# Attention row maxima: negated scores, and a second minimum that starts from the first one's value

## The chip, the cores and the metric

The kernel runs on one core of a Trainium2 chip. The metric is device time in microseconds (us), the median of several runs. Engines are named as in the profile: PE is TensorE's matmuls, PEld its weight loads, DVE VectorE, ACT ScalarE, POOL GpSimd, SP the engine that issues DMAs. A line such as L201 is a line of the kernel's source.

## The reference, cut to what matters

The reference is one layer of a backbone with two branches on the same normalised input: chunked gated linear attention, and differential attention. The change touches the second. For each of 8 heads there are two components, each with its own queries and keys (64 wide, normalised and rotated), and one value matrix. There are 1024 queries, and 1280 keys (256 of context, 1024 latent).

```python
scale = d ** -0.5                               # 1/8
s1 = jnp.einsum('bhqd,bhkd->bhqk', qb1, k1).astype(jnp.float32) * scale
s2 = jnp.einsum('bhqd,bhkd->bhqk', qb2, k2).astype(jnp.float32) * scale
a = jax.nn.softmax(s1, axis=-1) - lam * jax.nn.softmax(s2, axis=-1)
return jnp.einsum('bhqk,bhkv->bhqv', a.astype(v.dtype), v)
```

The queries are `rms_norm(q) * q_gain` before the rotation, so a factor on `q_gain` is a factor on every score. A softmax subtracts each row's maximum before the exponential; the maximum itself cancels from the result.

## The kernel before, in words

The program has three phases that overlap at their seams: A (projections and the linear attention, up to about 900 us), B (differential attention, about 900 to 1430 us) and C (the branch projections and the output, to the end).

**Order of the work.** The instructions of PE, ACT, DVE and POOL stand in an order that the program works out while it is built. A class `Driver` (from L59) keeps a clock for each engine and runs small tasks written as generators: each task yields a time, an event, or `On(t, engine)`, which holds it back until that engine's modelled queue is within a microsecond of free. Among tasks that are due, the lowest `prio` goes first. Each instruction on ACT, DVE and POOL is issued by `Engine.emit` (L201), which also gives it a modelled cost, so all of them bear that one line in the profile; matmuls are issued by `mm` (L349), transposes by `tr` (L375), DMAs by `dma` (L314). `banked` adds, for instructions that touch the same PSUM bank from different engines, a wait on the latest earlier one, and takes away waits between different banks. `acq` and `rel` hand out buffers by tag. The engines execute their lists in order. `att_order` writes out by hand the order on PE of the scores S, the transposes T of the exponentials and the product A with the values: the scores run four or five query tiles ahead, so that in the step in which a pair of tiles is multiplied by the values, scores are laid for the tiles that are five and six after the pair's first. Between them `fill` puts matmuls of other products (tile name mb), paced by how many query tiles have been scored.

**A query tile.** There are 64 of them (8 heads, 8 tiles of 128 queries). One PSUM buffer of five banks, `s5`, holds the scores of both components: component 0's first 1024 keys in banks 0 and 1 (main part), component 0's last 256 keys and component 1's first 256 in bank 2 (tail), component 1's other 1024 in banks 3 and 4 (main part). `att_scores` issues component 0's main matmuls, the two tails, and component 1's main matmuls, and spawns the following tasks:

- `att_max`, three times: a DVE reduction of a main part (128 x 1024 to 128 x 1) or of both tails at once (128 x 2 x 256 to 128 x 2), which gives the negated maximum.
- `att_exp`, once for each component: it waits for both reductions that bear on it, joins the two values with a minimum of 128 x 1 on DVE, and issues the ACT exponential of 1280 columns with the joined value as bias. The exponential also gives the row's sum `z`, and its end frees the component's banks for the next tile's scores.
- `att_mix`: after both exponentials, DVE works out the factor of component 1 and mixes the two (the 1280-column instruction e<-e,sm,e).

Afterwards `att_tr` transposes the mixed tile on PE, ACT, POOL and DVE split it into two parts (at), `att_av` multiplies by the values for two tiles at a time, and `att_fin` normalises the result (b1k) and stores it. The small buffers of 128 x 1 and 128 x 2 come from one ring, `sm`, of 48. Four are taken in `att_scores` for a tile (the tails' two maxima, the two main maxima, the sums), one in `att_mix`, and two in `att_fin` for two tiles.

**The gains.** `consts_late` loads the query norm weights and multiplies them by 0.125 on POOL, once, at the start of the program (L475). The rotation tables are multiplied by them later.

Of the kernel before, what the change touches and what calls it, by code (L numbers as in the profile page):

```python
# [13 lines left out]
AF = mybir.ActivationFunctionType  # L14
ALU = mybir.AluOpType
AX = mybir.AxisListType
# [4 lines left out]
P = 128  # L21
# [3 lines left out]
T = S + CTX  # L25
# [207 lines left out]
class Hybrid:  # L233
# [222 lines left out]
    def consts_late(self):  # L456

        nc, a = self.nc, self.a

        def bc(ap, n):  # L460
            return ap.unsqueeze(0).to_broadcast([P, n])

        self.gains = g = self.c("gains", [P, 2, 2, 64])
        for i, nm in enumerate(("diff_q_norm", "diff_k_norm")):
            self.dma(g[:, i, 0], bc(a[nm][0], 64))
        self.ggla = self.c("ggla", [P, 256])
        self.dma(self.ggla, bc(a["gla_norm"][0], 256))
        self.gdif = self.c("gdif", [P, P])
        self.dma(self.gdif, bc(a["diff_norm"][0], P))
        yield from self.acq("p", 2)  # L470
        lp = self.t("p", [P, 4, 64])
        self.dma(lp, a["diff_lambda"][0].unsqueeze(0).to_broadcast([P, 4, 64]))
        yield self.d.when(lp)

        self.pool.tensor_scalar(g[:, 0, 0], g[:, 0, 0], 0.125, 0.0, ALU.mult, ALU.add)  # L475
        for i in range(2):
            gi, gr = (g[:, i, x].rearrange("p (x h e) -> p x h e", h=2, e=16) for x in range(2))
            for hh in range(2):
                self.pool.tensor_scalar(gr[:, :, hh], gi[:, :, 1 - hh], 1.0, 0.0, ALU.mult, ALU.add)
        self.pool.tensor_scalar(self.ggla, self.ggla, 0.5, 0.0, ALU.mult, ALU.add)  # L480
        self.pool.tensor_scalar(self.gdif, self.gdif, 1.0 - LAM_INIT, 0.5, ALU.mult, ALU.mult)
        lm = self.t("p", [P, 2, 64])
        self.dve.tensor_tensor(lm, lp[:, 0::2], lp[:, 1::2], ALU.mult)
        ls = self.c("ls", [P, 2])
        self.rel("p", self.dve.tensor_reduce(ls, lm, AX.X, ALU.add), 2)
        yield self.d.when(ls)
        yield self.act.activation(ls, ls, AF.Exp)
        self.nlam = self.c("nlam", [P, 1])
        self.dve.tensor_tensor(self.nlam, ls[:, 1:2], ls[:, 0:1], ALU.subtract)
        self.dve.tensor_scalar(self.nlam, self.nlam, LAM_INIT, None, ALU.subtract)  # L490
# [1449 lines left out]
    def att_scores(self):  # L1940

        nc, d = self.nc, self.d
        yield self.ev_b
        s5 = self.t("s5", [P, 2 * T])
        for hd in range(8):
            for qt in range(8):
                pr, qs = qt // 2, slice((qt % 2) * P, (qt % 2) * P + P)
                yield self.ev_k[hd]
                yield self.ev_q[hd, pr]
                K, Q = self.K[hd], self.Q[hd, pr]  # L1950

                def score(po, comp, o, n):
                    bank = po.offset % (2 * T) // 512
                    for j in range(2):
                        e = self.mm(po, Q[comp][:, j, qs], K[comp][:, o:o + n], j == 0, j == 1)
                        self.banked(self.ins, "PE", bank)
                    return e

                u = dict(hd=hd, qt=qt, E=[None, None], mt=self.t("sm", [P, 2]), mx=[self.t("sm", [P, 1]) for _ in range(2)],
                         z=self.t("sm", [P, 2]), left=2, ev=[Event() for _ in range(3)])  # L1960

                for comp in range(2):
                    yield from self.acq(f"s{comp}")
                    pm = s5[:, 1536 * comp:1536 * comp + 1024]
                    if comp == 0:
                        yield from self.turn("S", 8 * hd + qt, 0)
                    if self.flush:
                        self.flush(1)
                    for x, (o, n) in enumerate(self.MAIN[comp]):
                        e = score(pm[:, x * 512:(x + 1) * 512], comp, o, n)  # L1970
                        if x == 0:
                            yield AtPE(0)
                    self.passed("S", 8 * hd + qt, comp)
                    d.spawn(self.att_max(u["ev"][comp], u["mx"][comp], pm, 3 * comp, 3 * comp + 1), On(e, "DVE"), prio=-3)
                    yield AtPE(0)
                    if comp == 0:
                        yield from self.acq("st")
                        yield from self.turn("S", 8 * hd + qt, 1)
                        pt = s5[:, 1024:1536].rearrange("p (c k) -> p c k", c=2)
                        for x in range(2):  # L1980
                            e = score(pt[:, x], x, *self.TAIL[x])
                        d.spawn(self.att_max(u["ev"][2], u["mt"], pt, 2), On(e, "DVE"), prio=-3)
                    elif qt == 7:
                        self.rel("kk", e, 2)
                    d.spawn(self.att_exp(u, comp, s5), On(e, "DVE"), prio=-3)
                    yield AtPE(0)
                if qt % 2 == 1:
                    self.rel(*(("aq", e, 2) if hd or pr else ("raw", e)))
                d.set(self.ev_u[8 * hd + qt])

    def att_max(self, ev, mx, pm, *banks):
        self.dve.tensor_reduce(mx, pm, AX.X, ALU.max, negate=True)
        self.banked(self.dve.ins, "DVE", *banks)
        self.d.set(ev)
        return
        yield

    def att_exp(self, u, comp, s5):
        d, mx = self.d, u["mx"][comp]
        yield u["ev"][2]  # L2000
        yield u["ev"][comp]
        yield d.on("DVE", mx)
        self.dve.tensor_scalar(mx, mx, u["mt"][:, comp:comp + 1], None, ALU.min)
        yield self.ev_sb
        yield from self.acq("e5")
        E = u["E"][comp] = self.t("e5", [P, T])
        yield d.on("ACT", mx)
        e = self.act.activation(E, s5[:, 1280 * comp:1280 * comp + T], AF.Exp, bias=mx, accum_out=u["z"][:, comp:comp + 1])
        self.banked(self.act.ins, "ACT", *range(2 * comp, 2 * comp + 3))
        self.rel(f"s{comp}", e)  # L2010
        u["left"] -= 1
        if u["left"] == 0:
            self.rel("st", e)
            if (u["hd"], u["qt"]) == (7, 7):
                d.set(self.ev_s2)
            d.spawn(self.att_mix(u), On(e, "DVE"), prio=self.PM)
# [794 lines left out]
```

## Time and profile before

| | |
|---|---|
| Time, median of 3 runs | 1617.41 us (1617.14 to 1617.72) |
| Span of the profiled execution, first to last instruction | 1614.1 us |
| That execution's own time | not listed; the median is 3.3 us above its span |
| PE busy over the span | 1591.4 us (99%) |
| PEld, DVE, ACT, POOL busy over the span | 82%, 76%, 52%, 39% |
| PE, DVE, ACT, POOL busy in the attention stage (900 to 1430 us) | 524.4, 441.4, 322.3, 323.9 us of 530 |
| Granted TensorE clock | 1.00 throughout |

How to read it: matmuls are pipelined and their ends are modelled, so PE counts as busy a little beyond the point at which the next matmul could have started, and a short wait of PE can be hidden in a busy share. Idle time of another engine costs nothing by itself. A wait is put down to the instruction that came last by the profile.

### The profile page before, as it was taken

The numbers are of one execution on the slowest core, as the hardware profiler recorded it, in microseconds if no ns is written. First come the engines' busy times: TensorE is split into PE (matmuls) and PEld (weight loads), VectorE is DVE, ScalarE is ACT, GpSimd is POOL, SyncE is SP. The second block draws the span as 40 slices with busy tenths as digits, with TensorE's granted clock in tenths as the row PEclk, the third lists the DMA queues.
The fourth block names the chain that finished last, engine by engine and source line by source line (L and its number), as shares of the span: only waits on it lengthen the run. The fifth ranks groups of instructions, "written<-read, shape, count | busy, mean of one in ns | idle before, by whom it ended". The sixth has DMA issues, their size and how long they took to land.

```text
span 1614.1 us, 24349 instructions
## 1 busy us (share of the span) xinstructions
PE 1591.4 (99%) x8229; PEld 1328.1 (82%) x8229; DVE 1224.4 (76%) x2118; ACT 835.7 (52%) x1720; POOL 634.3 (39%) x663
## 2 busy tenths in 40 slices
PE   8999999999999999999999999999999999999999
PEld 3788888888888888888888788888888888888887
DVE  4787945676777779767677688878778888888994
ACT  4776523435343454555535566665665666656331
POOL 1500000001415667535564256656765666560000
PEclk9999999999999999999999999999999999999999
DMA  8576996998878367564645944545587545347662
GB/s 305 201 257 239 329 304 232 344 331 295 278 238 281 116 194 235 167 212 118 189 118 158 253 121 121 151 129 151 150 264 218 159 137 150 111 155 285 204 206 100
DMA packets 259565, 331.16 MB, mean 205 GB/s; under 512 B 22600, under 2 KB 160752, under 8 KB 259440
## 3 DMA queue, kind: packets, MB, share of 16 engines
q1 hardware_dynamic: 259440, 329.60, 63.8%
q8 instruction: 65, 1.06, 0.3%
q14 instruction: 60, 0.49, 0.1%
HBM read 225.20 MB, written 104.33 MB: 204 GB/s over the span
## 4 chain that ended last, share of the span: by engine, by line
PE 89%; DVE 4%; issue 2%; DMA 2%; ACT 1%; POOL 1%; SPq 0%; ACTq 0%; DVEq 0%; POOLq 0%
PE mm L349 30%; PE mb L349 11%; PE s L349 8%; PE mc L349 7%; PE b L349 6%; PE tp L349 5%; PE gt L349 5%; PE b L375 5%; PE go L349 4%; PE gs L349 4%; PE mz L349 2%; PE tp L375 2%; DVE sm L201 1%; POOL at L201 1%; DMA w<-in_w_ada 1%
## 5 line engine op out<-in xcount | busy, mean ns | idle before, releaser
L349 PE MATMUL mm<-w,h 128*128 128x512 f32 x912 | 231.0, 400 | 0.0
L349 PE MATMUL mb<-h,wt 128*128 128x512 f32 x840 | 223.0, 400 | 0.0
L201 DVE TENSOR_REDUCE sm<-s 128x1 f32<-128x1024 f32 (+1 forms) x192 | 193.3, 1037 | 10.7 <-PE s L349 6.6
L201 ACT ACTIVATE e<-s,sm 128x1280 f32<-128x1280 f32 x128 | 169.3, 1329 | 54.4 <-DVE sm L201 51.2
L349 PEld LDWEIGHTS mm<-w,h 128*128 128x128 f32 x912 | 167.4, 188 | 32.8
L201 POOL TENSOR_TENSOR at<-ac,at 128x512 fp32r<-128x512 f32 x128 | 188.2, 1471 | 10.7
L349 PEld LDWEIGHTS mb<-h,wt 128*128 128x128 f32 x840 | 151.4, 188 | 28.6 <-DVE ft L201 0.3
L201 POOL TENSOR_SCALAR at<-ac 128x512 fp32r<-128x512 f32 x128 | 96.9, 757 | 191.0 <-ACT ac L201 190.7
L349 PE MATMUL s<-hk,aq 128*128 128x512 f32 x744 | 169.0, 363 | 1.9 <-ACT e L201 1.8
L349 PE MATMUL mm<-h,w 128*128 128x512 f32 x672 | 168.2, 400 | 1.0 <-DVE h L201 1.0
L349 PEld LDWEIGHTS mm<-h,w 128*128 128x128 f32 x672 | 123.7, 188 | 26.4 <-DVE h L201 1.5
L201 DVE TENSOR_TENSOR w<-raw,w 128x512 fp32r<-128x512 f32 x128 | 96.0, 766 | 54.2 <-ACT w L201 52.0
L349 PEld LDWEIGHTS s<-hk,aq 128*128 128x128 f32 x744 | 117.7, 189 | 18.5 <-ACT e L201 3.6
L349 PE MATMUL b<-at,vv 128*128 128x256 f32 x960 | 130.1, 287 | 1.1 <-ACT ac L201 0.8
L349 PEld LDWEIGHTS b<-at,vv 128*128 128x128 f32 x960 | 119.5, 191 | 2.8 <-ACT ac L201 1.0
L201 ACT ACTIVATE w<-raw 128x512 fp32r<-128x512 f32 x128 | 78.1, 626 | 84.2 <-PE tp L349 23.8
L201 ACT ACTIVATE ac<-b 128x512 f32<-128x512 f32 x122 | 72.5, 598 | 91.8 <-PE b L375 91.7
L201 POOL TENSOR_TENSOR sm<-sm,nhalf 128x2 f32<-128x2 f32 (+2 forms) x94 | 107.7, 1146 | 27.9 <-DVE sm L201 22.7
L201 DVE SCALAR_TENSOR_TENSOR e<-e,sm,e 128x1280 f32<-128x1280 f32 x64 | 117.9, 1842 | 1.0
L349 PE MATMUL mm<-w,g 128*128 128x512 f32 x432 | 105.7, 389 | 0.0
L349 PEld LDWEIGHTS mm<-w,g 128*128 128x128 f32 x432 | 81.1, 188 | 16.9
L375 PE MATMUL b<-ident,e 128*128 128x128 f32 x610 | 92.6, 273 | 1.3 <-ACT ac L201 0.8
(357 smaller groups left out, 3054.2 us busy)
## 6 DMA issues: line engine op xcount, KB each, us to landing
raw<-in_w_in SPq DMA_DIRECT2D x62, 512.0 KB, 4.3
g<-d_s SPq DMA_DIRECT2D x32, 640.0 KB, 6.2
g<-d_s SPq DMA_DIRECT2D x32, 512.0 KB, 5.7
aq<-d_qT SPq DMA_DIRECT2D x124, 128.0 KB, 3.4
d_dv<-pl SPq DMA_DIRECT2D x40, 256.0 KB, 3.9
gv<-d_v SPq DMA_DIRECT2D x40, 256.0 KB, 3.3
d_kT<-pl SPq DMA_DIRECT2D x40, 256.0 KB, 2.8
hk<-d_kT SPq DMA_DIRECT2D x32, 320.0 KB, 5.9
```

What stands on the lines that cost most here:

```text
L201: self.ins = f(out, *args, **kw).ins
L349: self.ins = self.nc.tensor.matmul(out, lhsT, rhs, start=start, stop=stop, skip_group_check=more).ins
L375: self.nc.tensor.transpose(out, src, self.ident[:n, :n])
```

## The change

The query gains are multiplied by -0.125 instead of 0.125, so that all scores come out negated; a row's maximum becomes a minimum of what stands in PSUM, which needs no negation, and the exponential takes the scores with a scale of -1.

Each component's minimum is now taken in two steps, of which the second starts from the first one's value. The first step is a plain reduction into `part`. The second is a DVE instruction that multiplies the scores by 1.0 and writes them back to their place in PSUM, while it accumulates a minimum that starts from `part`, and writes that to `mx`. Component 0 takes its main part first (1024 columns) and its tail second (256). Component 1 takes its tail first (256) and its main part second (1024). The tails are thereby two instructions of 256 columns instead of one of 512. The second step waits in the planner for the event of the first and for the time at which its value is ready on DVE. `att_exp` waits for the second step alone and has no instruction on DVE left. A tile takes five small buffers in `att_scores` instead of four.

```diff
-        self.pool.tensor_scalar(g[:, 0, 0], g[:, 0, 0], 0.125, 0.0, ALU.mult, ALU.add)
+        self.pool.tensor_scalar(g[:, 0, 0], g[:, 0, 0], -0.125, 0.0, ALU.mult, ALU.add)
...
-                u = dict(hd=hd, qt=qt, E=[None, None], mt=self.t("sm", [P, 2]), mx=[self.t("sm", [P, 1]) for _ in range(2)],
-                         z=self.t("sm", [P, 2]), left=2, ev=[Event() for _ in range(3)])
+                u = dict(hd=hd, qt=qt, E=[None, None], part=[self.t("sm", [P, 1]) for _ in range(2)],
+                         mx=[self.t("sm", [P, 1]) for _ in range(2)], z=self.t("sm", [P, 2]), left=2,
+                         ev=[Event() for _ in range(4)])
...
-                    d.spawn(self.att_max(u["ev"][comp], u["mx"][comp], pm, 3 * comp, 3 * comp + 1), On(e, "DVE"), prio=-3)
+                    d.spawn(self.att_max(u, comp, comp == 1, pm, 3 * comp, 3 * comp + 1), On(e, "DVE"), prio=-3)
...
-                        d.spawn(self.att_max(u["ev"][2], u["mt"], pt, 2), On(e, "DVE"), prio=-3)
+                        for x in range(2):
+                            d.spawn(self.att_max(u, x, x == 0, pt[:, x], 2), On(e, "DVE"), prio=-3)
...
-    def att_max(self, ev, mx, pm, *banks):
-        self.dve.tensor_reduce(mx, pm, AX.X, ALU.max, negate=True)
+    def att_max(self, u, comp, last, pm, *banks):
+        d, part = self.d, u["part"][comp]
+        if last:
+            yield u["ev"][comp]
+            yield d.on("DVE", part)
+            self.dve.tensor_scalar(pm, pm, 1.0, part, ALU.mult, ALU.min, accum_out=u["mx"][comp])
+        else:
+            self.dve.tensor_reduce(part, pm, AX.X, ALU.min)
         self.banked(self.dve.ins, "DVE", *banks)
-        self.d.set(ev)
-        return
-        yield
+        d.set(u["ev"][comp + 2 * last])
 
     def att_exp(self, u, comp, s5):
         d, mx = self.d, u["mx"][comp]
-        yield u["ev"][2]
-        yield u["ev"][comp]
-        yield d.on("DVE", mx)
-        self.dve.tensor_scalar(mx, mx, u["mt"][:, comp:comp + 1], None, ALU.min)
+        yield u["ev"][2 + comp]
         yield self.ev_sb
         yield from self.acq("e5")
         E = u["E"][comp] = self.t("e5", [P, T])
         yield d.on("ACT", mx)
-        e = self.act.activation(E, s5[:, 1280 * comp:1280 * comp + T], AF.Exp, bias=mx, accum_out=u["z"][:, comp:comp + 1])
+        e = self.act.activation(E, s5[:, 1280 * comp:1280 * comp + T], AF.Exp, bias=mx, scale=-1.0, accum_out=u["z"][:, comp:comp + 1])
```

## The prediction

> **What bounds the kernel now.** I read the summary, then the busy times by stage, the groups of the attention stage by shape, its waits, and two stretches of the timeline. First the summary and the stages (columns of the stage rows: length, then busy time and instructions of PE, PEld, DVE, ACT and POOL, granted clock, DMA share, GB/s).
>
> ```profile
> span 1614.1 us, 24349 instructions
> PE 1591.4 (99%) x8229; PEld 1328.1 (82%) x8229; DVE 1224.4 (76%) x2118; ACT 835.7 (52%) x1720; POOL 634.3 (39%) x663
> PE 89%; DVE 4%; issue 2%; DMA 2%; ACT 1%; POOL 1%; SPq 0%; ACTq 0%; DVEq 0%; POOLq 0%
> ```
>
> ```profile
> 900.00:1430.00 530.00, 524.42 (x3192) 454.95 (x3191) 441.43 (x809) 322.27 (x653) 323.88 (x288) 1.00 0.55 158
> 1380.00:1420.00 40.00, 39.99 (x246) 34.66 (x245) 36.19 (x65) 24.61 (x53) 21.40 (x23) 1.00 0.29 87
> 1420.00:1440.00 20.00, 19.67 (x129) 17.11 (x129) 19.06 (x28) 13.71 (x30) 15.59 (x13) 1.00 0.40 119
> ```
>
> Everything that the change touches, but for the one multiplication of the query gains, runs between 900 and 1430 us. There TensorE shows 524.4 of 530 us busy at full clock: 5.6 us idle. VectorE has 441.4 of 530 busy, 88.6 us to spare, or 1.38 us for each of the 64 query tiles (530 / 64 = 8.3 us each). Towards the end it has less: 3.8 us idle in the 40 from 1380 (4.8 tiles, 0.79 us each) and 0.9 us in the 20 after. So the stage is TensorE's, and only what TensorE loses by waiting can be won. The waits of the stage say how much, and on whom (last columns: total us, times, longest):
>
> ```profile
> ACT e L201 <- DVE sm L201: 51.2, 48, 3.4
> PEld s L349 <- ACT e L201: 4.3, 6, 1.8
> PE s L349 <- ACT e L201: 2.0, 3, 1.3
> PEld b L375 <- ACT ft L201: 1.5, 3, 0.5
> PEld b L375 <- ACT ac L201: 1.5, 3, 1.0
> PEld b L375 <- DVE at L201: 1.5, 3, 0.7
> PEld b L349 <- ACT ac L201: 1.0, 1, 1.0
> PEld b L375 <- DVE b1k L201: 0.5, 2, 0.3
> PEld mb L349 <- DVE ft L201: 0.3, 1, 0.3
> ```
>
> ScalarE's exponential (e) waits 51 us for maxima (sm), but of this TensorE sees little: its weight loads wait 4.3 us for the exponential, six times, and 6.3 us (1.5 + 1.5 + 1.5 + 1.0 + 0.5 + 0.3) for other work of ACT and DVE, 10.6 us in all. A weight load runs ahead of the matmuls, so these are upper bounds of what the matmuls lose.
>
> **The change part by part.** The groups of the stage by shape (busy us, mean ns of one, then idle before):
>
> ```profile
> L201 DVE TENSOR_REDUCE sm<-s 128x1 f32<-128x1024 f32 x128 | 155.7, 1216 | 10.7 <-PE s L349 6.6 <-ACT e L201 3.6
> L201 DVE SCALAR_TENSOR_TENSOR e<-e,sm,e 128x1280 f32<-128x1280 f32 x64 | 117.9, 1842 | 1.0
> L201 DVE TENSOR_REDUCE sm<-s 128x2 f32<-128x512 f32 x64 | 43.5, 680 | 0.0
> L201 DVE TENSOR_SCALAR sm<-sm,sm 128x1 f32<-128x1 f32 x186 | 31.9, 206 | 0.7
> L201 DVE SCALAR_TENSOR_TENSOR ft<-ft,mb 128x512 f32<-128x512 f32 x13 | 8.9, 682 | 5.9 <-PE mb L349 5.9
> L201 DVE RECIPROCAL sm<-sm 128x1 f32<-128x1 f32 x64 | 10.1, 158 | 26.2 <-ACT e L201 26.0
> L201 ACT ACTIVATE ac<-b 128x512 f32<-128x512 f32 x122 | 72.5, 598 | 91.8 <-PE b L375 91.7
> L201 ACT ACTIVATION_READ_ACCUMULATOR e<-s,sm 128x1 f32 x128 | 25.1, 196 | 0.0
> L201 ACT ACTIVATE ft<-mb 128x512 f32<-128x512 f32 x20 | 12.1, 606 | 4.3 <-PE mb L349 3.6 <-DMA aq<-d_qT 0.7
> ```
>
> Durations on VectorE overlap by pipeline latency, so I cost by starts. One tile of before and the row ahead of it, on DVE and on ACT:
>
> ```profile
> 1422.61 0.41 DVE L201 TENSOR_TENSOR at<-b,at 128x256 fp32r<-128x256 f32 x1
> 1422.94 2.94 DVE L201 TENSOR_REDUCE sm<-s 128x1 f32<-128x1024 f32 x3
> 1425.80 0.34 DVE L201 TENSOR_SCALAR sm<-sm,sm 128x1 f32<-128x1 f32 x2
> 1426.06 1.88 DVE L201 SCALAR_TENSOR_TENSOR e<-e,sm,e 128x1280 f32<-128x1280 f32 x1
> ...
> 1426.04 1.33 ACT L201 ACTIVATE e<-s,sm 128x1280 f32<-128x1280 f32 x1 [1.53 <-DVE sm L201]
> ```
>
> *Removed:* two 1024-column reduces, one 512-column reduce and two joining minima hold DVE from 1422.94 to 1426.06: 3.12 us a tile.
>
> *Added:* one 1024-column reduce, one of 256 columns, and two multiply-and-minimum instructions with an accumulator (256 and 1024 columns), which also write their scores back. A 1024-column pass holds DVE for 1.13 us (900.43 to 901.56, below), a 256-column one for 0.33 (1422.61 to 1422.94). A per-partition operand costs 0.05 (minimum 206 ns, reciprocal 158). So 2 x 1.13 + 2 x 0.33 + 2 x 0.05 = 3.02 us at the least, 0.10 a tile or 6 us in all below before.
>
> ```profile
> 900.43 1.22 DVE L201 TENSOR_REDUCE sm<-s 128x1 f32<-128x1024 f32 x1
> 901.56 0.68 DVE L201 TENSOR_TENSOR wt<-raw,wt 128x512 fp32r<-128x512 f32 x1
> ...
> 928.03 1.81 DVE L201 TENSOR_REDUCE sm<-s 128x1 f32<-128x1024 f32 x2
> 929.88 0.21 DVE L201 TENSOR_SCALAR sm<-sm,sm 128x1 f32<-128x1 f32 x1
> ```
>
> Three costs have no row of their own. (1) Reading out an accumulator: on ACT it is an instruction of 196 ns that delays the next by 0.08 us (905.45 to 905.53, further below); so 0 to 0.20 each, I take 0.08. (2) The second instruction reads the first one's value on the same engine; the minimum at 929.88 came 0.04 us after the reduces' end where an unbound one comes 0.08 before it: 0 to 0.12 each, I take half. (3) Writing 1024 + 256 columns back to PSUM: the best bound is the mixing pass, 1842 ns for 1280 columns, 1.44 ns a column against the reduce's 1.19: 0 to 0.32 us a tile; I take 0, because the 512-column pass that writes all its columns costs what the reduce does that writes two (682 and 680 ns), though its target is SBUF. Middle: 3.02 + 0.16 + 0.12 = 3.30, +0.18 a tile, +12 us of VectorE time; top: 3.02 + 0.40 + 0.24 + 0.32 = 3.98, +0.86 a tile, +55 us. TensorE's own work hides the middle: 0.18 is under the 0.79 that the tightest stretch has. Without that cover it would be 12 us.
>
> The Trainium skill, page "VectorE: DVE Perf Modes", section "Two Vector instructions with no wait between them", counts an operation that also writes out its accumulator as two instructions, the main one and an accumulator read; by that the five instructions of a tile become six, not four. No run here shows it yet; the sum by it lies between my middle and my top.
>
> *Moved:* what the exponential waits for. In the stretch above the planner put component 1's large reduce ahead of both joins, so exponential 0 started at 1426.04 though its inputs were reduced at 1424.67 (1422.94 + 1.13 + 0.60). Now its second minimum ends the matter: 1422.94 + 1.13 + 0.33 + 0.38 + 0.08 = 1424.86, and with the 0.24 us to ACT (1425.80 to 1426.04) it starts at 1425.10, 0.94 earlier. Exponential 1 keeps its place within 0.2 us: the same passes stand ahead of it. Queued behind the instruction that waits are only DVE's next passes: the mix, the transposes' remainders (at) and the branch scaling (b1k), each up to 0.12 later.
>
> *Worth nothing:* the sign in the gains is a number in a GpSimd instruction that ran anyway; the exponential's scale is a number too (606 ns with a scale, 598 for the copy without). Five instead of four small buffers a tile out of 48, beside two others, make the ring turn in 6.9 tiles instead of 8; by the written order a tile's sums are last read six tiles on, so I take 0 and keep a delay of one exponential (1.33 us) in the range. No DMA is added or moved.
>
> Who gains is the score matmul that waits for a score bank. The start of the stage has two of the six waits:
>
> ```profile
> 905.45 0.19 ACT L201 ACTIVATION_READ_ACCUMULATOR e<-s,sm 128x1 f32 x1
> 905.53 1.32 ACT L201 ACTIVATE e<-s,sm 128x1280 f32<-128x1280 f32 x1
> 905.68 0.76 PEld L349 LDWEIGHTS s<-hk,raw 128*128 128x128 f32 x4 [0.69 <-ACT e L201]
> ...
> 910.99 0.77 PEld L349 LDWEIGHTS s<-hk,aq 128*128 128x128 f32 x4 [1.76 <-ACT e L201]
> ```
>
> An exponential 0.94 earlier takes the first (0.69) whole and half of the second (0.9, since TensorE also gets there earlier). Of the other four (4.3 - 0.69 - 1.76 = 1.85) I take half, 0.9, as only those on component 0 gain. Against it 0.5 us for later remainders and scalings (they cost 1.5 + 0.5 + 0.3 now). **Sum: -0.7 - 0.9 - 0.9 + 0.5 = -2.0 us.** The span becomes 1612.1; 3.3 us lie around it (1617.4 is the runs' median, the page gives no total of its own): 1615.4.
>
> **The rivals.**
> *B, a clear gain:* the planner lays out the whole stage anew, with the score banks free up to a microsecond earlier, and ACT's and DVE's queues move up too. For it: 48 waits of exponentials for maxima. Against: 10.6 us is all there is to win, and most of it waits for work that the maxima don't precede. Taking 6 of the 10.6 gives 1611.4.
> *C, slower:* the accumulating instructions cost their top price and VectorE becomes the bound in the last 60 us of attention, where mixing, splitting for the next stage and maxima share it. It decides from 0.79 us a tile on; the top is 0.86. For it: VectorE at 36.2 of 40 and 19.1 of 20 us there. Against: it needs all three top prices. Price: five tiles x 0.86 = 4.3 us, less the 0.9 idle of the last 20, plus the 2.3 us of waits for DVE doubled: +5.7, 1623. The skill's two-instruction rule (above) speaks for its first price.
> *D, nothing:* the six waits only move to the next instruction, which is fill work paced by the planner, and TensorE's work is the same: 1617.4. The joins going away would then be real and unseen. For it: 99% busy.
>
> **How the numbers follow.** About 0.2%, 3.2 us, is what a measurement of this kernel can tell from no change: faster means under 1614.2, slower over 1620.6. My forecast has 0.44, B 0.27, C 0.14, D 0.15. Faster: B and 0.05 of the forecast's spread (a new layout moves the time by a few us whatever its cause), 0.32; slower: C and 0.03 from the same spread, 0.17; same 0.51. The range goes from B with two us more, about 1609.5, to just short of C, 1622: some 0.12 lies above, 0.06 below.
>
> **What would show it.** In the changed profile the 64 joins' pairs (sm<-sm,sm, 186 in the stage) fall by 128; exponentials' wait for sm falls from 51 us to under 25; the waits at 905.7 and 911 shrink by 0.7 and 0.9 us; accumulating passes of 1024 columns hold DVE 1.2 to 1.4 us, and VectorE's busy time in the stage rises by about 12 us. TensorE's idle in it falls from 5.6 to about 4. I am wrong if those passes hold DVE for over 1.7 us, if new waits for sm's buffers show, or if the exponential's wait halves and the time moves by more than 3 us, since then the layout and not the waits decided.

## The result, and the profile after

The changed kernel takes 1645.46 us (1645.30 to 1647.56, four runs) against 1617.28 (1616.03 to 1617.72, four runs beside it) for the kernel before: a ratio of 1.0178, 95% interval 1.0164 to 1.0193. That is 28 us slower, where 1615.4 was forecast.

From the summary of the changed kernel and its busy times by stage (columns as in the prediction):

```profile
span 1643.7 us, 24514 instructions
PE 1600.8 (97%) x8229; PEld 1329.4 (81%) x8229; DVE 1231.5 (75%) x2182; ACT 836.7 (51%) x1720; POOL 650.4 (40%) x663
PE 73%; DVE 12%; POOL 5%; issue 5%; ACT 3%; DMA 2%; SPq 0%; ACTq 0%; DVEq 0%; POOLq 0%
...
900.00:1430.00 530.00, 504.15 (x3081) 431.65 (x3080) 449.20 (x871) 324.39 (x660) 345.76 (x291) 1.00 0.52 149
```

TensorE is idle for 25.9 us of the stage that was 5.6 us idle before, and the chain of waits runs over PE for 73% of the span instead of 89%. TensorE's instruction count over the whole span is the same. From the waits of the same stage, after and then before:

```profile
ACT e L201 <- DVE s L201: 113.8, 60, 4.1
PE b L375 <- DVE b1k L201: 15.4, 19, 1.5
PEld b L375 <- ACT ac L201: 11.6, 15, 1.6
PEld b L375 <- DVE b1k L201: 7.9, 8, 1.7
PEld s L349 <- ACT e L201: 5.4, 8, 2.7
PE b L375 <- ACT ac L201: 4.3, 7, 1.4
```

```profile
PE b L375 <- DVE b1k L201: 1.1, 3, 0.4
```

The exponentials wait 113.8 us for maxima instead of 51.2. TensorE's new waits are in front of transposes, for DVE's work on the finished results (b1k: 15.4 us, 1.1 before) and for ACT's copies, and only a little for exponentials.

The decisive rows are of a kind that the prediction did not look at: how many fill matmuls (mb, then mc when the banks change) the program lays where, and when the last product with the values starts (the last time in each row is the last start). First before, then after:

```profile
L349 PE MATMUL b<-at,vv x960: 276/283/388, 931.7 to 1452.5; 128*128 128x256 f32 x192
L349 PE MATMUL mb<-h,wt x840: 387/393/501, 901.2 to 1506.7; 128*128 128x512 f32 x168
L349 PE MATMUL mc<-h,wt x72: 387/389/477, 1436.6 to 1503.9; 128*128 128x512 f32 x72
```

```profile
L349 PE MATMUL b<-at,vv x960: 276/283/386, 932.3 to 1449.4; 128*128 128x256 f32 x192
L349 PE MATMUL mb<-h,wt x696: 387/392/497, 903.9 to 1536.2; 128*128 128x512 f32 x174
L349 PE MATMUL mc<-h,wt x216: 387/389/478, 1434.9 to 1533.5; 128*128 128x512 f32 x108
```

840 + 72 and 696 + 216 are the same 912 matmuls: 144 have moved from mb to mc, from attention to behind it. (In the programs' own lists, 792 fill matmuls stand ahead of the last score before, 648 after; from the last product to the end the traces hold 700 and 844 matmuls. Both times it is again 144.) Attention ended only 3.1 us sooner (1449.4 against 1452.5), and what follows takes 1643.7 - 1449.4 = 194.3 us instead of 1614.1 - 1452.5 = 161.6: 32.7 us more, which is 0.227 us for each of the 144. 32.7 - 3.1 = 29.6 us is the difference of the spans. So TensorE waits in attention for nearly the time in which it did this fill before, and does the fill afterwards.

The new instructions themselves, in the timeline of DVE, and one wait of TensorE:

```profile
1092.64 1.22 DVE L201 TENSOR_REDUCE sm<-s 128x1 f32<-128x1024 f32 x1
1093.77 0.42 DVE L201 TENSOR_TENSOR at<-b,at 128x256 fp32r<-128x256 f32 x1
1094.10 0.41 DVE L201 TENSOR_REDUCE sm<-s 128x1 f32<-128x256 f32 x1
1094.55 0.49 DVE L201 TENSOR_SCALAR_CACHE_REDUCE s<-s,sm 128x256 f32<-128x256 f32 x1
1094.96 0.14 DVE L201 DVE_READ_ACCUMULATOR s<-s,sm 128x1 f32 x1
1095.22 1.29 DVE L201 TENSOR_SCALAR_CACHE_REDUCE s<-s,sm 128x1024 f32<-128x1024 f32 x1
1096.43 0.14 DVE L201 DVE_READ_ACCUMULATOR s<-s,sm 128x1 f32 x1
1096.43 0.42 DVE L201 TENSOR_TENSOR b1k<-b,b1k 128x256 f32<-128x256 f32 x1
...
1112.22 0.88 PE L375 MATMUL b<-ident,e 128*128 128x128 f32 x6 [1.20 <-DVE b1k L201]
```

An accumulating pass is two instructions, as the Trainium skill says in "VectorE: DVE Perf Modes", section "Two Vector instructions with no wait between them": the pass and a DVE_READ_ACCUMULATOR of 141 ns. From start to start a tile's four steps hold DVE for 1.13 (1092.64 to 1093.77) + 0.45 + 0.67 (1094.55 to 1095.22) + 1.21 (1095.22 to 1096.43) = 3.46 us, against 3.12 before.

### The profile page after: what moved, and what is told of

It reads as the page before. It is cut to its first block, busy times and chain, and to the rows that moved or that the text cites. A ratio compares the mean times of both kernels' runs of the same rounds, so it can differ in the third digit from the quotient of the medians.

```text
span 1643.7 us, 24514 instructions
## 1 busy us (share of the span) xinstructions
PE 1600.8 (97%) x8229; PEld 1329.4 (81%) x8229; DVE 1231.5 (75%) x2182; ACT 836.7 (51%) x1720; POOL 650.4 (40%) x663
## 4 chain that ended last, share of the span: by engine, by line
PE 73%; DVE 12%; POOL 5%; issue 5%; ACT 3%; DMA 2%; SPq 0%; ACTq 0%; DVEq 0%; POOLq 0%
PE mm L349 30%; PE mc L349 9%; PE tp L349 5%; PE gt L349 4%; PE mb L349 4%; PE go L349 4%; DVE sm L201 4%; PE gs L349 4%; PE s L349 3%; POOL at L201 3%; DVE e L201 3%; PE b L349 3%; DVE s L201 2%; PE mz L349 2%; PE b L375 2%
## 5 line engine op out<-in xcount | busy, mean ns | idle before, releaser
L201 ACT ACTIVATE e<-s,sm 128x1280 f32<-128x1280 f32 x128 | 170.3, 1331 | 115.5 <-DVE s L201 113.8
L349 PEld LDWEIGHTS mm<-w,h 128*128 128x128 f32 x912 | 167.4, 188 | 32.7
L201 POOL TENSOR_TENSOR at<-ac,at 128x512 fp32r<-128x512 f32 x128 | 189.5, 1480 | 10.7
L349 PE MATMUL mb<-h,wt 128*128 128x512 f32 x696 | 181.7, 399 | 0.0
L201 POOL TENSOR_SCALAR at<-ac 128x512 fp32r<-128x512 f32 x128 | 111.3, 869 | 122.3 <-ACT ac L201 120.0
L349 PEld LDWEIGHTS mb<-h,wt 128*128 128x128 f32 x696 | 125.9, 188 | 23.7
L201 POOL TENSOR_TENSOR sm<-sm,nhalf 128x2 f32<-128x2 f32 (+2 forms) x94 | 114.1, 1213 | 70.5 <-DVE sm L201 65.4
L201 DVE TENSOR_SCALAR_CACHE_REDUCE s<-s,sm 128x256 f32<-128x256 f32 (+1 forms) x128 | 114.2, 892 | 10.9 <-PE b L375 0.9
L201 DVE SCALAR_TENSOR_TENSOR e<-e,sm,e 128x1280 f32<-128x1280 f32 x64 | 120.1, 1877 | 1.4
L201 DVE TENSOR_REDUCE sm<-s 128x1 f32<-128x1024 f32 (+1 forms) x128 | 101.4, 811 | 6.0 <-PE s L349 5.8
L375 PEld LDWEIGHTS b<-ident,e 128*128 128x128 f32 x608 | 72.5, 141 | 37.1 <-ACT ac L201 8.3
```

What stands on the lines that cost most here:

```text
L201: self.ins = f(out, *args, **kw).ins
L349: self.ins = self.nc.tensor.matmul(out, lhsT, rhs, start=start, stop=stop, skip_group_check=more).ins
L375: self.nc.tensor.transpose(out, src, self.ident[:n, :n])
```

## The experiments

Two theories stood against each other at first. **L, the layout:** the planner, which works with its own prices, lays less fill into attention. **O, the operations:** accumulating passes are dear and the maxima come late.

### 1. The new instructions in the old order

PE, ACT and POOL have the instruction lists of the kernel before. The planner is charged for the old instructions (`d.op`), DVE is given the new ones.

```diff
+        if k == 0:
+            ins = [v.tensor_reduce(mt[:, 0:1], pm, AX.X, ALU.min).ins]
+        elif k == 1:
+            ins = [second(1, pm)]
+        else:
+            ins = [v.tensor_reduce(mt[:, 1:2], pm[:, 1], AX.X, ALU.min).ins, second(0, pm[:, 0])]
...
+        self.d.op("DVE", 0.07 + 0.00104 * pm.free_size(), [mt if k == 2 else mx[k]], [pm])
...
-        self.dve.tensor_scalar(mx, mx, u["mt"][:, comp:comp + 1], None, ALU.min)
+        self.d.op("DVE", 0.07 + 0.00104 * 0.5, [mx], [mx, u["mt"][:, comp:comp + 1]])
```

> The changed instructions in the order of the kernel before: PE, ACT and POOL have the list of the kernel before, instruction for instruction (792 fill matmuls ahead of the last score, against 648 in the changed kernel); on DVE the two accumulating passes stand where the tail's and component 1's reduces stood, and the joins are gone but stay in the planner's account. Theory L (the layout: the planner lays less fill into attention, and TensorE stands idle there) expects 1617 us within 4. Theory O (the operations: an accumulating pass with its read-out holds DVE some 0.35 us a tile longer and the maxima come late) expects most of the 28 us to stay, 1635 us or more.

Measured: 1617.91 us, ratio 1.0004 (0.9994 to 1.0013). Stage row, exponentials' wait, and the new rows by shape:

```profile
900.00:1430.00 530.00, 523.87 (x3184) 454.24 (x3185) 455.17 (x869) 322.03 (x651) 320.13 (x287) 1.00 0.54 159
...
ACT e L201 <- DVE s L1995: 19.5, 20, 2.6
...
L1995 DVE TENSOR_SCALAR_CACHE_REDUCE s<-s,sm 128x1024 f32<-128x1024 f32 x64 | 82.7, 1292 | 7.4
L1995 DVE TENSOR_SCALAR_CACHE_REDUCE s<-s,sm 128x256 f32<-128x256 f32 x64 | 31.5, 493 | 2.2
L1995 DVE DVE_READ_ACCUMULATOR s<-s,sm 128x1 f32 x128 | 18.2, 142 | 0.0
```

DVE's busy time rose by 13.7 us (441.4 to 455.2) and the exponentials' wait fell from 51.2 to 19.5, and the time is unchanged: under the old order the operations cost nothing and bring nothing. Theory O falls.

### 2. The old kind of instructions in the new order

```diff
-            self.dve.tensor_scalar(pm, pm, 1.0, part, ALU.mult, ALU.min, accum_out=u["mx"][comp])
+            v, mx = self.dve.eng, u["mx"][comp]
+            self.dve.ins = v.tensor_reduce(mx, pm, AX.X, ALU.min).ins
+            v.tensor_scalar(mx, mx, part, None, ALU.min)
+            d.op("DVE", 0.07 + 0.055 + 0.00104 * pm.free_size(), [pm, mx], [pm, part, mx])
```

> The mirror image: PE, ACT and POOL have the list of the changed kernel, instruction for instruction; each accumulating pass is replaced by a plain reduce and a 128x1 minimum with the first value, with no write back to PSUM. Theory L expects about 1640 us (1632 to 1650), since the layout is that of the changed kernel. Theory O expects 1617 to 1624.

Measured: 1643.61 us, ratio 1.0163 (1.0148 to 1.0179). Without any accumulating pass nearly the whole loss is there. The order carries it, and no accumulating pass is needed. This does not mean that DVE's time is indifferent: from start to start these instructions hold DVE for 1.13 + 2.29 = 3.42 us a tile (1095.79 to 1096.92 and 1097.25 to 1099.54 in the run's timeline), nearly the 3.46 of the changed kernel.

### 3. The kernel before, with joins that the planner does not know of

```diff
-        self.dve.tensor_scalar(mx, mx, u["mt"][:, comp:comp + 1], None, ALU.min)
+        self.dve.eng.tensor_scalar(mx, mx, u["mt"][:, comp:comp + 1], None, ALU.min)
```

> The kernel before with all its instructions, but the two joining minima are left out of the planner's account (no cost, no latency), so that it takes the exponentials to be ready about 0.3 us earlier than they are. It then lays 555 fill matmuls ahead of the last score instead of 792. Theory L expects a time like that of the changed kernel or worse: 28 us for 144 matmuls fewer is 0.19 us each, so 237 fewer give +46, 1645 to 1668. Theory O expects 1617 within 4, since no operation changes.

Measured: 1659.79 us, ratio 1.0261 (1.0245 to 1.0276), the slowest of all, with no instruction changed: it is enough that the planner believes the maxima to be ready sooner. The last product starts at 1441.9, 10.6 us sooner than before, and 1658.0 - 1441.9 = 216.1 us follow, 54.5 more: 237 matmuls at 0.23. TensorE's longest wait in this stage is for ACT's copies (10.6 us), not for DVE, so what a tighter layout runs into is not the same each time.

### 4. The changed kernel, with the measured prices in the planner

```diff
+            if self.name == "DVE" and acc:
+                c += 0.28 if n == 256 else 0.02
```

> The changed kernel, its instructions unchanged; only the planner's account gets the prices that the changed kernel's trace shows for the accumulating passes (0.67 us from start to start for 256 columns, 0.28 above the account; 1.21 for 1024, 0.02 above). It lays 762 fill matmuls ahead of the last score. Theory L expects 30 x 0.19 = 6 us above before: 1623 (1616 to 1629). Theory O expects 1640 or more.

Measured: 1627.48 us, ratio 1.0061 (1.0046 to 1.0076): 18 of the 28 us come back from two numbers in the account. The count of fill ahead of the last score asks for 6 us of loss, and 10 are left. The trace says why: from the start of the last product (1453.6) on, TensorE has 745 matmuls against 700 before, 45 more and not 30, and 45 x 0.227 = 10.2 us is what the stretch behind that point takes more (171.8 against 161.6).

### 5 and 6. Both kernels without the mixing pass

Why does attention not run faster when less work is laid into it? The next runs take DVE's largest pass away. Its cost stays in the planner's account, so the orders stay. The result lacks the second component.

```diff
-            e = self.dve.scalar_tensor_tensor(E[0], E[1], cf, E[0], ALU.mult, ALU.add)
+            e = d.op("DVE", 0.07 + 0.055 + T * 0.00104, [E[0]], [E[1], cf, E[0]])
```

> The changed kernel in its own order (648 fill matmuls ahead of the last score; PE, ACT and POOL lists the same), but the 1280-column mixing pass on DVE (1.88 us a tile, a quarter of DVE's time in the stage) is not issued; it stays in the planner's account. The second component is thereby left out of the result. If DVE's queue is what holds a tile at 8.1 us where the plan asks for less (theory D), attention falls to the plan's pace and the time to 1605 to 1622 us. If the way from the transposes over ACT and POOL back to PE holds it (theory R), it stays at 1638 or more.

> The control for the run without the mixing pass: the kernel before, in its own order, also without the pass (the second component is left out of the result). TensorE is the bound of its attention stage, so both theories expect little: at most the 10 us for which TensorE waits there, 1607 to 1617 us.

Measured: 1616.57 us for the changed kernel (ratio 0.9989, 0.9979 to 0.9999) and 1614.35 for the one before (0.9979, 0.9970 to 0.9988). The products with the values in the changed order, without the mix:

```profile
L349 PE MATMUL b<-at,vv x960: 277/283/369, 929.7 to 1421.1; 128*128 128x256 f32 x192
```

With DVE relieved, the changed order's last product starts at 1421.1, 28 us sooner, and the loss is gone; the old order gains 3 us, about 0.2%. TensorE's wait for b1k falls from 15.4 to 2.6 us. The exponentials still wait 73.3 us for maxima, more than the 51.2 of the kernel before, so their wait by itself is not the loss. The holes were holes of DVE, or of something that the mixing pass disturbs.

### 7. The changed kernel, with a step that does not exist in the planner's account

```diff
+        yield d.on("DVE", mx)
+        d.op("DVE", 0.3, [mx], [mx])
```

> The changed kernel with its instructions; the planner alone is told of a step of 0.3 us on DVE between a maximum and its exponential, which does not exist. It lays 795 fill matmuls ahead of the last score. Theory L expects 1617 us within 4 (before has 792); the theory that the operations count expects 1640 or more.

Measured: 1620.85 us, ratio 1.0021 (1.0012 to 1.0031). The instructions are those of the changed kernel; believing its maxima late wins back 25 of the 28 us. The other 3 lie ahead of the last product (it starts at 1457.9 against 1452.5, and 161.7 us follow against 161.6); they are not explained.

### 8. The kernel before, with more fill in attention

```diff
-        self.dve.tensor_scalar(mx, mx, u["mt"][:, comp:comp + 1], None, ALU.min)
+        self.dve.eng.tensor_scalar(mx, mx, u["mt"][:, comp:comp + 1], None, ALU.min)
+        d.op("DVE", 0.07052 + 0.5, [mx], [mx, u["mt"][:, comp:comp + 1]])
```

> The kernel before with all its instructions; the planner alone takes the joining minima for 0.5 us longer than they were, and lays 852 fill matmuls ahead of the last score instead of 792. Theory L in its plain form (0.19 us for each matmul of fill) expects 60 x 0.19 = 11 us less, 1606. If fill only helps until TensorE has no gap left (theory S, saturation), it expects 1613 to 1619, with attention longer and the stage behind it shorter by the same.

Measured: 1650.17 us, ratio 1.0199 (1.0184 to 1.0214). Both expectations miss: more fill than before is as bad as less. A wait of its attention (900 to 1480), and the 120 us around its end, here and then in the kernel before:

```profile
PE b L375 <- ACT ac L201: 12.3, 16, 0.8
...
1430.00:1550.00 120.00, 104.52 (x526) 86.66 (x525) 91.65 (x164) 62.88 (x133) 33.55 (x30) 0.91 0.49 169
```

```profile
1430.00:1550.00 120.00, 118.95 (x573) 99.58 (x572) 107.50 (x180) 56.17 (x117) 19.47 (x16) 1.00 0.73 247
```

TensorE waits 12.3 us for ACT's copies inside attention; at the end it is 14.4 us more idle than before (118.95 - 104.52), and its clock there is 0.91 in the mean, at most another 9% of 120, 10.8 us, since the two can fall together. The places of the loss can be told by the last product, which starts at 1485.9, 33.4 us later than before. From there on TensorE has 633 matmuls against 700, so 67 x 0.227 = 15.2 us of fill have gone into attention: 18.2 of the 33.4 are loss there. The rest takes 163.1 us where 161.6 - 15.2 = 146.4 would do: 16.7 are loss behind it. Together that is the 34.9 us between the spans. So theory L in its plain form, a price for each matmul of fill, does not hold above the kernel before. That the end is bare because the fill is used up is my reading; no run adds it back there.

### 9. The mixing pass replaced by a reduce of the same width

The result lacks the mix here and in the run after the next.

```diff
-            e = self.dve.scalar_tensor_tensor(E[0], E[1], cf, E[0], ALU.mult, ALU.add)
+            self.dve.eng.tensor_reduce(cf, E[0], AX.X, ALU.max)
+            e = d.op("DVE", 0.07 + 0.055 + T * 0.00104, [E[0]], [E[1], cf, E[0]])
```

> The changed kernel in its own order (648 fill matmuls; PE, ACT and POOL lists the same); the mixing pass is replaced by a plain 1280-column reduce of the first component's exponentials on DVE, which holds DVE but reads one tensor. The mix is thereby left out of the result. The planner's account of a tile's DVE work is then short by about 0.4 us (the accumulating passes) instead of 0.8 (these and the mix, which takes 1.88 us against 1.46 in the account). Theory G (what counts is how far DVE's real time a tile lies above the planner's account) expects about half of the 28 us to go: 1624 to 1636. If DVE's bare occupancy counts, however accounted, 1638 or more; if the pass's reading of two tensors beside GpSimd was the whole matter, 1614 to 1622.

Measured: 1622.48 us, ratio 1.0022 (1.0013 to 1.0032). This is just below what theory G expects, at the edge of the third expectation. Two things changed at once: DVE's pass takes 1483 ns instead of 1877, and GpSimd's passes are shorter (more on that at the end). The rows, here and then in the changed kernel:

```profile
L2032 DVE TENSOR_REDUCE sm<-e 128x1 f32<-128x1280 f32 x64 | 94.9, 1483 | 1.3
...
L201 POOL TENSOR_TENSOR at<-ac,at 128x512 fp32r<-128x512 f32 x128 | 165.7, 1295 | 10.7
L201 POOL TENSOR_SCALAR at<-ac 128x512 fp32r<-128x512 f32 x128 | 86.5, 675 | 146.7 <-ACT ac L201 133.1 <-PE b L349 9.1 <-PE s L349 2.2
```

```profile
L201 DVE SCALAR_TENSOR_TENSOR e<-e,sm,e 128x1280 f32<-128x1280 f32 x64 | 120.1, 1877 | 1.4
...
L201 POOL TENSOR_TENSOR at<-ac,at 128x512 fp32r<-128x512 f32 x123 | 183.0, 1488 | 10.3
L201 POOL TENSOR_SCALAR at<-ac 128x512 fp32r<-128x512 f32 x123 | 107.3, 873 | 119.0 <-ACT ac L201 118.4 <-PE b L349 0.6
```

### 10. A layout between

```diff
+            if self.name == "DVE" and acc:
+                c += 0.2
```

> The changed kernel with its instructions; the planner alone takes each accumulating pass for 0.2 us longer. It lays 690 fill matmuls ahead of the last score, between the changed kernel's 648 (1645 us) and the priced one's 762 (1627 us). Theory L expects a time between the two, by the fill about 1638 (1632 to 1643). If the planner's price itself counted, and not the layout that comes of it, it would be nearer to the priced kernel: 1632 or less.

Measured: 1642.33 us, ratio 1.0146 (1.0129 to 1.0163): in the stated interval, near its end. A price of 0.2 for each pass, 0.4 a tile, leaves the layout, and the time, nearly as they were; 0.28 for the small pass and 0.02 for the large (run 4), 0.3 a tile, does not. So the time goes by the layout and not by the price. It does not go by the fill alone: behind the last product 184.8 us follow, 9.5 less than in the changed kernel, as 42 x 0.227 asks, but that product starts 6.2 us later (1455.6 against 1449.4). TensorE's clock falls four times in this attention (0.57 over the 4 us from 1068, for one) and once in the changed kernel's; 0.43 x 4 = 1.7 us each, an estimate from the granted clock, would make 5.2 of the 6.2 us. Theory G fares badly: this account is 0.4 us a tile nearer to the chip, as it is in run 9, and 3 us come back instead of 23.

### 11. The same, with DVE held as long as by the mix

```diff
             self.dve.eng.tensor_reduce(cf, E[0], AX.X, ALU.max)
+            self.dve.eng.tensor_reduce(cf, E[0][:, :320], AX.X, ALU.max)
```

> The changed kernel in its own order, with the mixing pass replaced by two plain reduces of 1280 and 320 columns, which hold DVE together about as long as the mix did (1.80 us from start to start) but read one tensor at a time, so that GpSimd's passes stay at their undisturbed 1.30 and 0.68 us. The mix is left out of the result. If DVE's queue is what the layout runs into (theory D), the time goes back to 1637 us or more from the 1622 of the single reduce. If it was the mix's and GpSimd's hold on each other (theory P), it stays at 1628 or less. In between, both count.

Measured: 1641.50 us, ratio 1.0143 (1.0126 to 1.0159). GpSimd is as undisturbed as in run 9, DVE as long at work as with the mix:

```profile
900.00:1430.00 530.00, 508.59 (x3091) 435.19 (x3090) 453.05 (x934) 323.75 (x660) 286.20 (x293) 0.99 0.52 149
...
L201 POOL TENSOR_TENSOR at<-ac,at 128x512 fp32r<-128x512 f32 x124 | 161.3, 1301 | 10.4
L2033 DVE TENSOR_REDUCE sm<-e 128x1 f32<-128x320 f32 x64 | 31.1, 486 | 2.2
```

One reduce of 486 ns a tile (31 us in all, its overlap included) costs 19 us (1641.50 against 1622.48). It is time on DVE that this layout runs into, and not the hold on GpSimd.

## Why the prediction was wrong, point by point

**The step that failed** is "TensorE's own work hides the middle". It took TensorE's list for the stage, with the fill in it, as given, and asked only what could be won from the 10.6 us of waits in it. But that cover is laid by the planner, from modelled times that the change alters: it charges 1.13 + 1.19 + 0.34 + 0.39 = 3.05 us a tile for the new steps (their formula in `Engine.emit`), nearly what it charged before (3.01), and lets the exponential follow without a join. The chip takes 3.46. Believing the maxima to be sooner, the planner packs attention more tightly, with 144 fewer fill matmuls: 144 x 0.227 / 64 = 0.51 us of TensorE work less a tile. DVE does not follow at that pace, so TensorE waits: 25.9 us idle in the stage instead of 5.6. That the belief is enough is shown by runs 3 and 7, that the operations alone do nothing by run 1, that time on DVE is what the changed layout runs into by runs 5, 9 and 11. DVE is not full there, though: it is busy for 449.2 of the 530 us. It works through its list in order and itself waits for exponentials (33.2 us) and for GpSimd (16.7 us of b1k), so the idle share of DVE, 88.6 us, on which the prediction counted, was no measure of what could be added in the new layout. Which of these waits closes the loop is not shown. Why the planner's belief takes out 144 matmuls and not 30 is open; runs 4 and 10 show only that it jumps.

**Rival B** saw that the planner would lay out the stage anew, and gave that one sign: a gain. **Rival C** had the right sign and the right engine, but another mechanism and place: it asked for top prices (0.86 us a tile; it is 0.34) and for the last 60 us. The loss is spread over the stage: in pieces of 65 us from 895 on TensorE stands idle for 2.6 to 4.8 us in each of the first seven, and for 1.2 and 1.0 in the last two, up to 1480. **Rival D**, nothing happens, is what the operations do in run 1.

**What the terms of the sum were.** DVE's cost was near: 3.30 us a tile in the middle, 3.46 measured, +12 us of busy time against +13.7 in run 1. Of its three open prices, writing back to PSUM is next to nothing (1292 ns against 1212 for the plain reduce, of which 50 are the operand's). The read-out is an instruction of 0.14 us, but an independent one starts together with it (1096.43), so behind the large pass read-out and write-back hold DVE for 1.21 - 1.13 - 0.05 = 0.03 us, where 0.08 was taken for the read-out alone. The dear part is the waiting of one step for another, which was put at 0.06 each. The small pass starts 0.04 us after the end of the reduce ahead of it, which thereby holds DVE for 0.45 instead of 0.33. The large pass starts 0.12 us after the end of the small one's read-out, so that the small pass holds 0.67 instead of 0.33 + 0.05 + 0.08 = 0.46. The reduce ahead of the small pass is the other component's, whose value the small pass does not read; what it waits for the trace does not name.

The exponential does come earlier, but only in run 1 (19.5 us of waits, "under 25" was named as the sign). In the changed kernel it waits 113.8 us. The -2.5 us for score matmuls did not come even in run 1: it measures +0.3 us, -1.0 to +2.1 by its interval. No wait for the ring of small buffers shows in either trace. The sign of the gains and of the scale cost nothing, as said (both are in run 1).

**The test in the prediction**, that "the layout and not the waits decided", was the right one to name, but it asked that the exponential's wait halves and the time moves by more than 3 us. The wait doubled. A new layout belonged among the rivals with both signs, not with the waits as its condition.

## What to carry to other kernels

Where a program orders its instructions by a model of the chip, a change has two effects: what the new instructions cost, and what the model makes of them. Before trusting a busy engine as cover, compare how much work of each kind the two programs lay into the stage. Then run the new instructions in the old order and the old ones in the new order; these two runs alone showed that it was the order. Prices taken from start to start, read-outs and waits included, mend much of it but not all: in run 4 they brought back 18 of the 28 us.

## What the runs showed of the hardware that was not expected

**A wait of TensorE of little more than 2 us can be followed by half clock.** At the start of attention the changed kernel's scores wait 2.29 us for an exponential, those of the kernel before 1.34. The first 256-column scores after it (timeline, then the 8 us around; the granted clock is the third number from the end), after and then before:

```profile
914.35 1.20 PE L349 MATMUL s<-hk,aq 128*128 128x512 f32 x4 [2.29 <-ACT e L201]
915.76 2.93 PE L349 MATMUL s<-hk,aq 128*128 128x256 f32 x8 [0.21 <-ACT e L201]
...
912.00:920.00 8.00, 5.49 (x23) 4.37 (x23) 6.39 (x13) 5.06 (x8) 0.00 (x0) 0.79 1.17 306
```

```profile
910.99 1.20 PE L349 MATMUL s<-hk,aq 128*128 128x512 f32 x4 [1.34 <-ACT e L201]
914.07 1.56 PE L349 MATMUL s<-hk,aq 128*128 128x256 f32 x8
...
909.00:917.00 8.00, 6.66 (x35) 5.36 (x34) 7.54 (x11) 4.22 (x7) 0.21 (x1) 1.00 0.99 274
```

After the longer wait the eight matmuls take 2.93 us instead of 1.56, and the granted clock is 0.79 instead of 1.00. The Trainium skill, "TensorE: Matmul & The Clock Gate", section "What's actually happening", gives two clocks, half and full, and a drop to half after an idle window of about 3.4 us; the half agrees (0.50 in run 4 from 1436 to 1440), but here a wait of 2.29 us was enough. The length of the wait is not the whole rule either. At the same place a wait of 2.20 us in run 9 and one of 2.23 in run 2 left the clock at 1.00, and the eight matmuls took 1.67 and 1.66 us; one of 2.27 in run 10 and one of 2.73 in run 11 did not (granted clock 0.57 and 0.63 from 914 to 918). What else decides is open.

**Two engines that read the same memory slow each other, and that was not the cause.** GpSimd's two passes over a split tile take 1488 and 873 ns in the mean in the changed kernel, where a third or so of them run beside the mix, and 1295 and 675 with a reduce in its place (run 9). The mix in turn takes 1.54 to 1.55 us in the four tiles of the changed kernel in which it overlaps no such pass of GpSimd, and 1.91 in the mean of the 58 in which it overlaps one for half a microsecond or more. The Trainium skill, "SBUF — State Buffer", section "Who interferes with whom", says that a DVE instruction with two SBUF inputs contends with a GpSimd instruction that reads SBUF, and that a reduce never contends; these rows agree. Run 11 keeps GpSimd undisturbed and loses the time all the same.
